# Forgetting attention with values stationary and heads on column halves; memory attention with three buffers, taken ahead of banks; a planner cost for accumulator reads

## The chip, the cores and the metric

One core of a Trainium2 chip runs the whole program in one launch. The metric is the device time of one execution in microseconds (us).

## The reference, cut to what matters

Three mixers, each followed by a gated feed-forward block, all in float32, on 256 tokens of width 1024 (one batch). Mixers 0 and 1 hold a main attention (retention, differential attention) beside a *memory attention*; mixer 2 holds a state-space part (SSD) beside the *forgetting attention* ("fox"). The two attentions that the change touches:

```python
def memory_attention(qc, mk, mv):            # 4 heads of 64, 256 memory rows; mixers 0 and 1
    sc = jnp.einsum('bshd,bmhd->bhsm', qc, mk) * (qc.shape[-1] ** -0.5)
    p = jax.nn.softmax(sc, axis=-1)
    return jnp.einsum('bhsm,bmhd->bshd', p, mv)

def fox_mixer(q, k, v, f_raw, ...):          # 16 heads of 64; mixer 2
    ...
    for start in range(0, s, Q_BLOCK):       # two query blocks of 128; keys 0:end
        logits = jnp.einsum('bhqd,bhkd->bhqk', qh[:, :, start:end], kh[:, :, :end]) * scale
        logits = logits + cum[:, :, start:end, None] - cum[:, :, None, :end]
        p = jax.nn.softmax(jnp.where(causal, logits, -jnp.inf), axis=-1)
        outs.append(jnp.einsum('bhqk,bhkd->bhqd', p, vh[:, :, :end]))

x = x + jnp.concatenate([o_main, o_mem], axis=-1) @ w_out[layer]     # mixers 0, 1
x = x + jnp.concatenate([y_ssd, y_fox], axis=-1) @ w_out_2           # mixer 2
```

## The kernel before, in words

**Work of TensorE.** Nearly all of it is products of activations with weights. Each is done as three matmuls of 512 columns in fp32r, on numbers that are split into a high and a low part: `wh` by `lth`, `wl` by `lth`, `wh` by `ltl`. A unit of weights is loaded into a stage `st` (4 buffers), cast on ScalarE (ACT) to `wh` (6 buffers), and subtracted on VectorE (DVE) to `wl`; the stage is free after that, and the next load into it is issued on SyncE. `lth` is a rounded copy of the activations made on ACT, `ltl` the rest made on DVE (`split`, L293). These matmuls, here called main matmuls, run back to back; the attentions' small matmuls (plain f32) are put between them. The stages are mixer 0, feed-forward 0, mixer 1, feed-forward 1, mixer 2, feed-forward 2; each mixer ends in an output projection (`w_out`, L958), which goes over pieces of 128 rows of the concatenated heads in the orders OUT0 = OUT1 = (4, 6, 0, 2) and OUT2 (L1304). A number in these lists is the first of two neighbouring pieces, so the memory heads (6, 7) come second of four in mixers 0 and 1.

**What sets the order.** A planner in Python (`Weave`, L102) writes one fixed sequence for each engine. Pieces of work are generators; the planner keeps a clock for each engine from the costs in `cost` (L116), and starts a generator's next step when its inputs are done on these clocks and its buffers (`yield ring, n`) are free. Casts of weights are put in as `fill` (L382). On the chip each engine runs its sequence strictly in order, and semaphores hold it where the inputs are late. So the costs decide the order alone, and a wait on the chip stops all that stands behind it on that engine. Every operation is recorded by one helper at L89, so the rows tell lines apart by names: `psm` (3 banks) and `psa` (5 banks) are PSUM.

**Memory attention** (`mem_attn`, L686). For each of two blocks of 128 queries: scores into two `psa` banks, two maxima on DVE, four exps on ACT with the row sums as `accum_out` into `mp` (ring of 2), four scalings on ACT by the reciprocal sums, eight transposes in two banks and two copies to `mpT` on ACT. Block 1 is started 2.5 us after block 0 by the planner's clock. After both, the values `mv` are the stationary operand and `mpT` streams 256 columns; the two heads of a pair write partitions 0 to 63 and 64 to 127 of one bank, that is, they take the two column halves of the array. The bank is split into `lth` and `ltl`, which the output projection reads as pieces 6 and 7.

**Forgetting attention** (`fox`, L1406, once for each half of the 16 heads). A `pair` of heads makes two `att`, one for each query block: scores, mask, maxima, exps with `accum_out` into `pr`, transposes (2 for the first block, 4 for the second), a copy to `pT`, then two or four matmuls with `pT` stationary and 64 columns of `vv` streaming, and a DVE multiply by the reciprocal sums into `fy`. When all four pairs are done, `fy` is transposed (4 for each token block), and split into `lth`/`ltl` in pieces of 512 columns.

Of the kernel before, what the change touches and what calls it, by code (L numbers as in the profile page):

```python
# [9 lines left out]
AF = mybir.ActivationFunctionType  # L10
ALU = mybir.AluOpType
# [3 lines left out]
P = 128  # L15
# [84 lines left out]
class Weave:  # L100
# [15 lines left out]
    def cost(self, key, op, args, kw, aps):  # L116
        n = max(a.size() // a.shape[0] if callable(a.size) else a.size // a.shape[0] for a in aps[:2])
        if key == "T":
            if op == "transpose":
                return 109  # L120
            return n / 2.4 + 3 if args[2].dtype == F32R else max(n / 0.6, 104) + 3
        if key == "V":
            return 65 + 1.05 * n + 60 * any(a.size() == a.shape[0] if callable(a.size) else a.size == a.shape[0] for a in aps[1:])
        if key == "S":
            c = 45 + 0.88 * n + 93 * sum(isinstance(kw.get(k), bass.AP) for k in ("bias", "scale", "accum_out"))
            func = args[2] if op == "activation" else None
            if func in (AF.Exp, AF.Silu) and func != self.table:
# [95 lines left out]
def _build(tc, a, out, stop):  # L223
# [462 lines left out]
    def mem_attn(l, mx, got, kvt, qc, oT, mpr):  # L686
# [14 lines left out]
        pT = mx.tile([P, 2, 4, 256], F32, tag="mpT", name=W.name("mpT"))  # L701

        def block(t):
            yield psa, 2
            sc = [psa.get(True), psa.get(True)]
            for p in range(2):
                for j in range(2):
                    T.matmul(sc[j][:, p * 256 : (p + 1) * 256], qT[64 * j : 64 * j + 64, p, t * P : (t + 1) * P],
                             kT[64 * j : 64 * j + 64, p, :], start=True, stop=True)
            prs = []  # L710
            yield
            for j in range(2):
                mxv = small([P, 2])
                V.tensor_reduce(mxv, sc[j][:].rearrange("p (j m) -> p j m", j=2), axis=AX.X, op=ALU.max)
                V.tensor_scalar(mxv, mxv, -0.125, None, op0=ALU.mult)
                yield mpr, 1
                pr = mpr.get(True)
                for p in range(2):
                    S.activation(pr[:, p * 256 : (p + 1) * 256], sc[j][:, p * 256 : (p + 1) * 256], AF.Exp,
                                 bias=mxv[:, p : p + 1], scale=0.125, accum_out=sums[:, t, 2 * p + j : 2 * p + j + 1])  # L720
                psa.close(sc[j])
                prs.append(pr)
            yield
            rs = small([P, 4])
            V.reciprocal(rs, sums[:, t, :])
            yield
            for j in range(2):
                for p in range(2):
                    cols = slice(p * 256, (p + 1) * 256)
                    S.activation(prs[j][:, cols], prs[j][:, cols], AF.Copy, scale=rs[:, 2 * p + j : 2 * p + j + 1])  # L730
            yield
            for j in range(2):
                yield psa, 1
                tp = psa.get(True)
# [273 lines left out]
    def mixer0(H, nxt, first):  # L1008
# [2 lines left out]
        w = a["w_in"][0]  # L1011
        u, E, oT = {}, {}, {}
        dtab = mx.tile([P, 6, 384], F32, name="dtab")
        sTr, hsq, onr, mpr = ring(mx, 384, "sT", 3), ring(mx, 512, "hsq", 1), ring(mx, 512, "on", 3), ring(mx, 512, "mp", 2)
        sqm[0] = ring(mx, 256, "sqm", 2)

        def chunk(c, ev, first=None):
# [112 lines left out]
    def mixer1(H, nxt, kv1):  # L1130
# [3 lines left out]
        oT, u, qkT, E = {}, {}, {}, {}  # L1134
        btab = mx.tile([P, 384], F32, name="btab")
        uqr, sqg, pdr, aTr = ring(mx, 512, "uq", 4), ring(mx, 512, "sqg", 1), ring(mx, 384, "pd", 6), ring(mx, 384, "aT", 5)
        hsq, onr, mpr = ring(mx, 512, "hsq", 1), ring(mx, 512, "on", 2), ring(mx, 512, "mp", 2)
        sqm[0] = ring(mx, 256, "sqm", 1)

        def chunk(c, serial=False):  # L1140
# [165 lines left out]
    def mixer2(H, nxt):  # L1306
# [11 lines left out]
        uxr = ring(mx, 1024, "ux", 2)  # L1318
        augr = {(i, t): ring(mx, (8, 66), f"aug{i}{t}", 1) for i in range(2) for t in range(2)}
        fTr = [Ring(W, mx, [66, 2, 256], F32, f"fT{i}", 2) for i in range(2)]  # L1320
        vvr, fyr, prr, pTr = ring(mx, 512, "vv", 2), ring(mx, 512, "fy", 2), ring(mx, 512, "pr", 3), ring(mx, 512, "pT", 2)
        tbr, dcr = ring(mx, 512, "tb", 1), ring(mx, 512, "dc", 4)
        aT = mx.tile([32, P], F32, name="aT")
        am = Ring(W, scr_pool, [32, P], F32, "am", 1).get(True)
# [80 lines left out]

        def fox(f, aug, deps, vv, got_v, pace):  # L1406
            sums = small([P, 2, 8], "f", 2)
            ys = [fyr.get(True) for _ in range(2)]

            def att(hp, ib, qT, kT):  # L1410
                nj = (ib + 1) * P
                yield psa, 1
                sc = psa.get(True)
# [13 lines left out]
                                 bias=mxv[:, j : j + 1], scale=0.125,  # L1427
                                 accum_out=sums[:, ib, 2 * hp + j : 2 * hp + j + 1])
                psa.close(sc)
                yield psa, 1  # L1430
                nb = 2 * (ib + 1)
                tp = psa.get(True)
                transposes(tp, blocks(pr, nb))
                prr.close(pr)
                yield pTr, 1
                pT = pTr.get(True)
                S.copy(pT[:, : nb * P], tp[:, : nb * P])
                psa.close(tp)
                yield psa, 1
                o = psa.get(True)  # L1440
                for j in range(2):
                    h = 2 * hp + j
                    for kb in range(ib + 1):
                        T.matmul(o[:, j * 64 : (j + 1) * 64], pT[:, (j * (ib + 1) + kb) * P : (j * (ib + 1) + kb + 1) * P],
                                 vv[kb][:, h * 64 : (h + 1) * 64], start=kb == 0, stop=kb == ib)
                pTr.close(pT)
                rs = small([P, 2])
                V.reciprocal(rs, sums[:, ib, 2 * hp : 2 * hp + 2])
                yield
                V.tensor_tensor(g64(ys[ib][:, 2 * hp * 64 : (2 * hp + 2) * 64]), g64(o[:, :P]), bcast(rs, 64), op=ALU.mult)  # L1450
                psa.close(o)
                yield

            def pair(hp):
# [15 lines left out]
                        for t in range(2):  # L1470
                            augr[which, t].close(aug[which][t])
                yield
                a0 = go(att(hp, 0, *qk))
                yield pace / 3
                a1 = go(att(hp, 1, *qk))
                yield [a0, a1]
                for which in range(2):
                    fTr[which].close(qk[which])

            yield deps + [got_v]  # L1480
            hs = []
# [2 lines left out]
                yield pace  # L1484
            yield hs
            vvr.close(*vv)
            lts = []
            for t in range(2):
                yield psa, 1
                ps = psa.get(True)  # L1490
                transposes(ps, blocks(ys[t]))
                fyr.close(ys[t])
                yield
                lt = yield from lt_tiles()
                yield from split(lt[0][:], lt[1][:], ps[:])
                psa.close(ps)
                lts.append(lt)
                for b in range(4):
                    oT[8 + 4 * f + b, t] = tuple(z[:, b * P : (b + 1) * P] for z in lt)
            yield  # L1500
            return lts


        def xbc_proj(i):
# [384 lines left out]
```

## Time and profile before

| | |
|---|---|
| median of 3 runs | 1014.52 us (1013.83 to 1016.05) |
| the profiled execution's own time | 1014.46 us |
| its span, first to last instruction | 1012.5 us |
| busy: PE, DVE, ACT, POOL | 99%, 67%, 61%, 7% of the span |

A row of the trace's timeline gives the start, the duration and the number of instructions of one kind in a run. Neighbouring matmuls overlap in their records, so the time that one takes from the engine is read as the distance from its start to the start of the next row, here called its step; the same holds for neighbouring rows of ACT. An f32 matmul is recorded as two passes.

### The profile page before, as it was taken

How to read it: one execution, taken by the hardware profiler on the slowest of the kernel's cores; microseconds unless marked ns; L12 is line 12 of the kernel's file. 1: busy time of each engine (PE TensorE's matmuls, PEld its weight loads, DVE VectorE, ACT ScalarE, POOL GpSimd, SP SyncE). 2: the span in 40 equal slices, each digit the busy share in tenths (PEclk: the TensorE clock that was granted, in tenths of full speed). 3: DMA queues.
4: the chain of work that ended last, by engine and by line, in shares of the span. 5: the costliest groups of instructions: out<-in, count | busy, mean ns of one | idle time of the engine just before them, and what ended most of it. 6: DMA issues, size and time to landing. Idle time of an engine off the chain costs nothing.

```text
span 1012.5 us, 13836 instructions
## 1 busy us (share of the span) xinstructions
PE 1002.2 (99%) x4994; PEld 832.4 (82%) x4994; DVE 678.1 (67%) x1026; ACT 622.5 (61%) x1001; POOL 69.8 (7%) x93
## 2 busy tenths in 40 slices
PE   8999999999999999999999999999999999999998
PEld 6887888888898777788888888888888888888887
DVE  5675666555556877756565477778767667878775
ACT  7558654443455887644445356688778557767853
POOL 1121000000001231100000001100400010000000
PEclk9999999999999999999999999999999999999999
DMA  7763566776564433677677457633632659877743
GB/s 250 261 222 105 183 208 212 252 229 193 179 227 155 146 104 107 208 247 233 203 229 239 137 152 220 215 104 104 210 125 84 208 164 289 262 232 240 247 156 116
DMA packets 121780, 193.79 MB, mean 191 GB/s; under 512 B 8400, under 2 KB 39920, under 8 KB 121584
## 3 DMA queue, kind: packets, MB, share of 16 engines
q1 hardware_dynamic: 121712, 192.92, 59.9%
q8 instruction: 39, 0.64, 0.3%
q14 instruction: 29, 0.24, 0.1%
HBM read 183.43 MB, written 9.45 MB: 191 GB/s over the span
## 4 chain that ended last, share of the span: by engine, by line
PE 91%; ACT 2%; DVE 2%; DMA 2%; POOL 2%; issue 1%; SPq 0%; ACTq 0%; DVEq 0%
PE psm L89 60%; PE psa L89 31%; POOL s8r L89 1%; DMA xt<-x 1%; ACT pd L89 1%; DMA dc<-am 1%; DMA st<-w_gate_up 1%; DVE wl L89 0%; DVE pd L89 0%; DVE s L89 0%; ACT wh L89 0%; POOL s4r L89 0%; POOL s16r L89 0%; SPq L259 0%; ACT qkT L89 0%
## 5 line engine op out<-in xcount | busy, mean ns | idle before, releaser
L89 DVE TENSOR_TENSOR wl<-st,wh 128x1024 fp32r<-128x1024 f32 (+2 forms) x339 | 388.4, 1166 | 195.4 <-ACT wh L89 194.5
L89 ACT CAST wh<-st 128x1024 fp32r<-128x1024 f32 (+2 forms) x339 | 334.5, 1007 | 223.9 <-PE psm L89 84.0
L89 PE MATMUL psm<-wh,lth 128*128 128x512 f32 (+2 forms) x1024 | 395.2, 386 | 1.1 <-ACT lth L89 1.1
L89 PE MATMUL psm<-wl,lth 128*128 128x512 f32 (+2 forms) x1024 | 385.6, 377 | 0.0
L89 PE MATMUL psm<-wh,ltl 128*128 128x512 f32 (+2 forms) x1024 | 381.0, 377 | 0.3 <-DVE ltl L89 0.2
L89 PEld LDWEIGHTS psm<-wh,ltl 128*128 128x128 f32 x1024 | 192.6, 188 | 36.8 <-DVE ltl L89 0.9
L89 PEld LDWEIGHTS psm<-wh,lth 128*128 128x128 f32 x1024 | 192.8, 188 | 35.8 <-issue 2.0
L89 PEld LDWEIGHTS psm<-wl,lth 128*128 128x128 f32 x1024 | 192.9, 188 | 32.6 <-DVE wl L89 0.7
L89 PE MATMUL psa<-wh,lth 128*128 128x512 f32 x328 | 130.7, 398 | 0.0
L89 PE MATMUL psa<-wl,lth 128*128 128x512 f32 x328 | 127.9, 390 | 0.0
L89 PE MATMUL psa<-wh,ltl 128*128 128x512 f32 x328 | 105.1, 390 | 0.0
L89 PEld LDWEIGHTS psa<-wh,ltl 128*128 128x128 f32 x328 | 61.6, 188 | 13.2
L89 PEld LDWEIGHTS psa<-wh,lth 128*128 128x128 f32 x328 | 61.6, 188 | 12.4 <-ACT lth L89 0.3
L89 PEld LDWEIGHTS psa<-wl,lth 128*128 128x128 f32 x328 | 61.7, 188 | 12.0 <-issue 0.2
L89 POOL TENSOR_SCALAR s1n<-s1n 128x1 f32<-128x1 f32 x14 | 5.6, 402 | 461.6 <-ACT sq L89 461.4
L89 DVE SCALAR_TENSOR_TENSOR cc<-na,ccol,cc 128x255 f32<-128x255 f32 (+1 forms) x64 | 27.4, 480 | 7.4 <-ACT cc L89 7.2
L89 ACT ACT_TABLE_LOAD x20 | 25.7, 1283 | 7.8 <-DMA dc<-am 2.8
L89 DVE SCALAR_TENSOR_TENSOR sg<-psm,s1n,sg 128x512 f32<-128x512 f32 (+1 forms) x24 | 16.9, 705 | 19.5 <-PE psm L89 19.3
L89 ACT ACTIVATE uu<-psm,s1n 128x512 f32<-128x512 f32 (+1 forms) x24 | 15.6, 652 | 18.3 <-PE psm L89 18.2
L89 ACT ACTIVATE sg<-psm,s1n 128x512 f32<-128x512 f32 (+1 forms) x24 | 15.7, 653 | 17.9 <-PE psm L89 17.7
L89 ACT ACTIVATE sq<-xt 128x512 f32<-128x512 f32 x24 | 15.2, 634 | 18.2 <-DVE xt L89 17.7
L89 POOL TENSOR_TENSOR s16r<-s16r,mhalf 128x16 f32<-128x16 f32 x7 | 22.2, 3166 | 0.6
(213 smaller groups left out, 829.3 us busy)
## 6 DMA issues: line engine op xcount, KB each, us to landing
st<-w_gate_up SPq DMA_DIRECT2D x80, 512.0 KB, 4.6
st<-w_in SPq DMA_DIRECT2D x67, 512.0 KB, 4.3
st<-w_down SPq DMA_DIRECT2D x66, 512.0 KB, 5.5
st<-w_up SPq DMA_DIRECT2D x40, 512.0 KB, 4.8
st<-w_out SPq DMA_DIRECT2D x32, 512.0 KB, 3.9
scr<-sq SPq DMA_DIRECT2D x64, 128.0 KB, 4.8
fl<-scr SPq DMA_DIRECT2D x16, 512.0 KB, 5.9
st<-w_in SPq DMA_DIRECT2D x30, 256.0 KB, 3.8
```

What stands on the lines that cost most here:

```text
L89: f(*args, **kw)
```

## The change

- In `cost`, an ACT operation with `accum_out` counts 110 ns more. It alters no instruction, only the planner's clock and so the order, in all stages.
- Memory attention: the `mp` ring has three buffers in place of two, and a block takes its two `mp` buffers first and its two score banks after that. Before, it took the banks first and each buffer after the maxima.
- Forgetting attention: the probabilities are scaled by the reciprocal sums on ACT (two instructions for each `att`) before they are transposed, `pT` holds both query blocks of a pair (768 columns, ring of three), and one set of matmuls for a pair has the values stationary and streams `pT`: 256 columns with the first 128 keys, 128 columns with the second, the two heads on the two column halves. Its result is the transposed one, so the `fy` multiplies on DVE and the 16 `fy` transposes are gone; it is split into `lth`/`ltl` in pieces of 256 columns.

```diff
@@ cost
             c = 45 + 0.88 * n + 93 * sum(isinstance(kw.get(k), bass.AP) for k in ("bias", "scale", "accum_out"))
+            c += 110 * ("accum_out" in kw)
@@ mem_attn, block(t)
+            yield mpr, 2
+            prs = [mpr.get(True), mpr.get(True)]
             yield psa, 2
             sc = [psa.get(True), psa.get(True)]
...
-                yield mpr, 1
-                pr = mpr.get(True)
+                pr = prs[j]
@@ mixer0, mixer1
-        hsq, onr, mpr = ring(mx, 512, "hsq", 1), ring(mx, 512, "on", 2), ring(mx, 512, "mp", 2)
+        hsq, onr, mpr = ring(mx, 512, "hsq", 1), ring(mx, 512, "on", 2), ring(mx, 512, "mp", 3)
@@ mixer2
-        vvr, fyr, prr, pTr = ring(mx, 512, "vv", 2), ring(mx, 512, "fy", 2), ring(mx, 512, "pr", 3), ring(mx, 512, "pT", 2)
+        vvr, prr, pTr = ring(mx, 512, "vv", 2), ring(mx, 512, "pr", 3), ring(mx, 768, "pT", 3)
@@ fox, att(hp, ib, qT, kT, pT)
+                rs = small([P, 2])
+                yield
+                V.reciprocal(rs, sums[:, ib, 2 * hp : 2 * hp + 2])
+                yield
+                for j in range(2):
+                    S.activation(pr[:, j * nj : (j + 1) * nj], pr[:, j * nj : (j + 1) * nj], AF.Copy, scale=rs[:, j : j + 1])
                 yield psa, 1
...
-                        T.matmul(o[:, j * 64 : (j + 1) * 64], pT[:, (j * (ib + 1) + kb) * P : (j * (ib + 1) + kb + 1) * P],
-                                 vv[kb][:, h * 64 : (h + 1) * 64], start=kb == 0, stop=kb == ib)
-                V.tensor_tensor(g64(ys[ib][:, 2 * hp * 64 : (2 * hp + 2) * 64]), g64(o[:, :P]), bcast(rs, 64), op=ALU.mult)
@@ fox, pair(hp)
+                        T.matmul(o[64 * j : 64 * j + 64, kb * P : 256], vv[kb][:, (2 * hp + j) * 64 : (2 * hp + j + 1) * 64],
+                                 pT[:, 384 * j + 256 * kb : 384 * j + 256 + 128 * kb], start=kb == 0, stop=kb == 1)
...
+                yield from split(lt[0][:, at : at + 256], lt[1][:, at : at + 256], o[:, :256])
@@ fox, end
-                transposes(ps, blocks(ys[t]))
-                yield from split(lt[0][:], lt[1][:], ps[:])
```

How the order moves is shown at three places, in rows as they stand in the fixed sequence of an engine; a name ends in a number that tells its buffers apart, `x2` means two like instructions.

The first is ACT in the output projection of mixer 0, from the last two copies of the transposed memory probabilities (`mpT`) on. Before (`lth_1152` is the memory heads' operand, `lth_1146` and `lth_1169` are the retention heads'):

```order
L89 COPY mpT_931<-psa_1107 128x4x128
L89 CAST wh_1117<-st_898 128x1024
L89 CAST wh_1119<-st_920 128x1024
L89 ACTIVATE lth_1146<-psa_1127,pcol 128x2x128 x2
L89 CAST lth_1152<-psa_1132 128x512
L89 ACTIVATE lth_1169<-psa_1141,pcol 128x2x128 x2
L89 CAST wh_1176<-st_947 128x1024
```

With the change (`lth_1198` is the memory heads' operand):

```order
L89 COPY mpT_931<-psa_1153 128x4x128
L89 CAST wh_1178<-st_949 128x1024
L89 CAST wh_1182<-st_1089 128x1024
L89 CAST wh_1188<-st_1137 128x1024
L89 CAST wh_1194<-st_1141 128x1024
L89 CAST lth_1198<-psa_1169 128x512
```

On PE at the same place the sequence now is:

```order
L89 MATMUL psa_1153<-pcol,mp_1022 128x128 x4
L89 MATMUL psa_1093<-wh_932,lth_874 128x512
L89 MATMUL psa_1169<-mpT_931,mv_577 64x256 x2
L89 MATMUL psa_1169<-mpT_931,mv_578 64x256 x2
L89 MATMUL psm_1091<-wh_1101,lth_1198 128x512
```

Six main matmuls with `wh_932` and `wh_1066` lie between the first and the third of these rows (one of them is shown). Before, twelve main matmuls and four transposes stood between the value matmuls and the first use of the memory heads' `lth`; now none stands there, and four weight casts stand ahead of `lth` on ACT.

The second is the same place of mixer 1, on ACT, with the change (`pd` is the differential attention's probabilities, `aT` their transposed difference; `lth_3769` is the memory heads' operand):

```order
L89 COPY mpT_3437<-psa_3690 128x4x128
L89 ACTIVATE pd_3681,s4s_3670<-pd_3681,s_830_3669 128x128
L89 ACTIVATE pd_3683,s4s_3670<-pd_3683,s_830_3669 128x256
L89 COPY mpT_3437<-psa_3714 128x4x128
L89 COPY aT_3729<-psa_3724 128x384
L89 CAST wh_3731<-st_3505 128x1024
L89 CAST wh_3733<-st_3532 128x1024
L89 CAST wh_3748<-st_3607 128x1024
L89 CAST wh_3754<-st_3702 128x1024
L89 ACTIVATE pd_3681<-pd_3681,s4s_3670 128x128
L89 ACTIVATE pd_3681<-pd_3681,s4s_3670 128x256
L89 CAST lth_3769<-psa_3737 128x512
```

Two more exps of `pd` lie between the two copies to `mpT`. Before, the copies were followed by 10 exps and scalings of `pd` and an evacuation of `u`, and `lth` came ahead of the next casts, with 24 main matmuls on PE between the value matmuls and its first use. On PE the value matmuls are now followed by seven transposes and then by the first main matmul that reads `lth_3769`.

The third is ACT in mixer 2's first half, with the change (`zs` are gates of the SSD part, `cv` its convolution, `pr` the forgetting attention's probabilities):

```order
L89 CAST wh_6355<-st_6138 128x1024
L89 ACTIVATE zs_6175<-psm_6177,s1n_5422 128x512
L89 ACTIVATE pr_6371,s16f_5996<-psa_6349,s_1407_6362 128x128 x2
L89 ACTIVATE zs_6176<-psm_6189,s1n_5531 128x512
L89 ACTIVATE pr_6402,s16f_5996<-psa_6368,s_1412_6381 128x256 x2
L89 CAST wh_6408<-st_6184 128x1024
L89 ACTIVATE pr_6443,s16f_5996<-psa_6399,s_1425_6416 128x128 x2
L89 CAST wh_6450<-st_6243 128x1024
L89 ACTIVATE pr_6371<-pr_6371,s_1410_6374 128x128 x2
L89 ACTIVATE pr_6402<-pr_6402,s_1421_6405 128x256 x2
```

A table load stands at each of the three switches between `zs` and `pr`. Before, the cast for the same unit of weights stood ahead of the convolution's activations and of both `zs`; now it stands behind them.

## Rows read from the trace of the kernel before

**Rows 1.** The page: busy time, the granted TensorE clock by slices of the span, and the chain that ended last.

```profile
PE 1002.2 (99%) x4994; PEld 832.4 (82%) x4994; DVE 678.1 (67%) x1026; ACT 622.5 (61%) x1001; POOL 69.8 (7%) x93
PEclk9999999999999999999999999999999999999999
PE 91%; ACT 2%; DVE 2%; DMA 2%; POOL 2%; issue 1%; SPq 0%; ACTq 0%; DVEq 0%
```

**Rows 2.** What PE waited for, in the whole span: us in total, times, longest.

```profile
PE psm L89 <- ACT lth L89: 1.1, 1, 1.1
PE psa L89 <- DVE u L89: 1.0, 1, 1.0
PE psa L89 <- DVE pd L89: 0.3, 1, 0.3
PE psa L89 <- DVE on L89: 0.2, 1, 0.2
```

**Rows 3.** Timeline of PE in mixer 2: start, duration, operation, count.

```profile
668.25 0.55 PE L89 MATMUL psa<-vv,pT 128*128 128x64 f32 x4
668.61 0.48 PE L89 MATMUL psm<-wh,lth 128*128 128x512 f32 x1
669.83 1.00 PE L89 MATMUL psa<-vv,pT 128*128 128x64 f32 x8
670.66 0.61 PE L89 MATMUL psa<-pcol,ux 128*128 128x128 f32 x4
...
698.14 1.02 PE L89 MATMUL psa<-tb,bct 128*128 128x512 f32 x2
699.00 0.60 PE L89 MATMUL psa<-pcol,fy 128*128 128x128 f32 x4
699.36 0.47 PE L89 MATMUL psm<-wh,lth 128*128 128x512 f32 x1
```

**Rows 4.** Timeline of PE in the output projection of mixer 0, around the memory attention's value matmuls.

```profile
106.18 0.60 PE L89 MATMUL psa<-pcol,on 128*128 128x128 f32 x4
106.71 1.95 PE L89 MATMUL psa<-mpT,mv 128*64 128x256 f32 x16
108.59 0.66 PE L89 MATMUL psa<-pcol,on 128*128 128x128 f32 x4
109.00 0.47 PE L89 MATMUL psa<-wh,lth 128*128 128x512 f32 x1
...
111.85 0.39 PE L89 MATMUL psm<-wh,lth 128*128 128x512 f32 x1
```

**Rows 5.** Timeline of ACT there; in brackets the idle time ahead and what ended it.

```profile
104.99 0.59 ACT L89 COPY mpT<-psa 128x512 f32<-128x512 f32 x1 [0.65 <-PE psa L89]
105.47 1.99 ACT L89 CAST wh<-st 128x1024 fp32r<-128x1024 f32 x2
107.37 0.84 ACT L89 ACTIVATE lth<-psa,pcol 128x256 fp32r<-128x256 f32 x2
108.71 0.59 ACT L89 CAST lth<-psa 128x512 fp32r<-128x512 f32 x1 [0.50 <-PE psa L89]
109.28 0.84 ACT L89 ACTIVATE lth<-psa,pcol 128x256 fp32r<-128x256 f32 x2
110.01 2.00 ACT L89 CAST wh<-st 128x1024 fp32r<-128x1024 f32 x2
113.76 1.05 ACT L89 CAST wh<-st 128x1024 fp32r<-128x1024 f32 x1 [1.75 <-DMA st<-w_out]
```

**Rows 6.** Timeline of ACT in the output projection of mixer 1.

```profile
386.03 0.42 ACT L89 ACTIVATE pd<-pd,s 128x128 f32<-128x128 f32 x1
...
387.80 0.68 ACT L89 ACTIVATE u<-psm,s1n 128x512 f32<-128x512 f32 x1
...
391.00 0.78 ACT L89 ACTIVATE pd<-pd,s4s 128x128 f32<-128x128 f32 x2
391.69 0.56 ACT L89 CAST lth<-psa 128x512 fp32r<-128x512 f32 x1
...
395.22 0.85 ACT L89 COPY aT<-psa 128x384 f32<-128x384 f32 x2
```

**Rows 7.** Busy time by windows of mixer 2's attention stage (us; windows with their length, then PE, PEld, DVE, ACT, POOL, granted clock, DMA share, GB/s).

```profile
650.00:675.00 25.00, 25.00 (x155) 21.45 (x154) 16.42 (x44) 22.24 (x48) 0.00 (x0) 1.00 0.23 68
675.00:700.00 25.00, 25.00 (x144) 21.02 (x144) 20.95 (x46) 22.67 (x44) 0.00 (x0) 1.00 0.36 104
700.00:725.00 25.00, 24.91 (x133) 20.98 (x132) 20.71 (x33) 17.89 (x32) 5.90 (x6) 1.00 0.53 158
725.00:750.00 25.00, 24.87 (x135) 20.50 (x134) 16.16 (x42) 16.66 (x34) 5.25 (x4) 1.00 0.64 202
750.00:775.00 25.00, 25.00 (x148) 21.36 (x148) 20.19 (x47) 23.63 (x48) 0.00 (x0) 1.00 0.28 97
775.00:800.00 25.00, 25.00 (x137) 20.94 (x136) 19.21 (x31) 15.10 (x27) 0.98 (x2) 1.00 0.42 140
```

**Rows 8.** Timeline of ACT in mixer 0 (the scalings of the memory attention) and in mixer 2 (the cast of a unit of weights), and of PE at that unit's first use.

```profile
99.56 1.71 ACT L89 ACTIVATE mp<-mp,s 128x256 f32<-128x256 f32 x4
101.29 1.28 ACT L89 ACT_TABLE_LOAD   x1
...
680.32 1.04 ACT L89 CAST wh<-st 128x1024 fp32r<-128x1024 f32 x1
...
697.36 0.48 PE L89 MATMUL psm<-wh,lth 128*128 128x512 f32 x1
```

More of the change, by code (lines that the diff above doesn't have):

```diff
@@ L709, in block @@
                              kT[64 * j : 64 * j + 64, p, :], start=True, stop=True)
-            prs = []
             yield
@@ L721, in block @@
                 psa.close(sc[j])
-                prs.append(pr)
             yield
@@ L1013, in mixer0 @@
         dtab = mx.tile([P, 6, 384], F32, name="dtab")
-        sTr, hsq, onr, mpr = ring(mx, 384, "sT", 3), ring(mx, 512, "hsq", 1), ring(mx, 512, "on", 3), ring(mx, 512, "mp", 2)
+        sTr, hsq, onr, mpr = ring(mx, 384, "sT", 3), ring(mx, 512, "hsq", 1), ring(mx, 512, "on", 3), ring(mx, 512, "mp", 3)
         sqm[0] = ring(mx, 256, "sqm", 2)
@@ L1407, in fox, with att @@
             sums = small([P, 2, 8], "f", 2)
-            ys = [fyr.get(True) for _ in range(2)]
-            def att(hp, ib, qT, kT):
+            lts = {}
+            def att(hp, ib, qT, kT, pT):
                 nj = (ib + 1) * P
@@ L1429, in att @@
                 psa.close(sc)
[L1430 to L1443, printed above, removed]
-                        T.matmul(o[:, j * 64 : (j + 1) * 64], pT[:, (j * (ib + 1) + kb) * P : (j * (ib + 1) + kb + 1) * P],
-                                 vv[kb][:, h * 64 : (h + 1) * 64], start=kb == 0, stop=kb == ib)
-                pTr.close(pT)
                 rs = small([P, 2])
+                yield
                 V.reciprocal(rs, sums[:, ib, 2 * hp : 2 * hp + 2])
                 yield
-                V.tensor_tensor(g64(ys[ib][:, 2 * hp * 64 : (2 * hp + 2) * 64]), g64(o[:, :P]), bcast(rs, 64), op=ALU.mult)
-                psa.close(o)
+                for j in range(2):
+                    S.activation(pr[:, j * nj : (j + 1) * nj], pr[:, j * nj : (j + 1) * nj], AF.Copy, scale=rs[:, j : j + 1])
+                yield psa, 1
+                tp = psa.get(True)
+                transposes(tp, blocks(pr, 2 * (ib + 1)))
+                prr.close(pr)
+                S.copy(pT[:].rearrange("p (j n) -> p j n", j=2)[:, :, ib * P : ib * P + nj],
+                       tp[:, : 2 * nj].rearrange("p (j n) -> p j n", j=2))
+                psa.close(tp)
                 yield
@@ L1472, in pair @@
                 yield
-                a0 = go(att(hp, 0, *qk))
+                yield pTr, 1
+                pT = pTr.get(True)
+                a0 = go(att(hp, 0, *qk, pT))
                 yield pace / 3
-                a1 = go(att(hp, 1, *qk))
+                a1 = go(att(hp, 1, *qk, pT))
                 yield [a0, a1]
@@ L1478, in pair @@
                     fTr[which].close(qk[which])
+                yield psa, 1
+                o = psa.get(True)
+                for kb in range(2):
+                    for j in range(2):
+                        T.matmul(o[64 * j : 64 * j + 64, kb * P : 256], vv[kb][:, (2 * hp + j) * 64 : (2 * hp + j + 1) * 64],
+                                 pT[:, 384 * j + 256 * kb : 384 * j + 256 + 128 * kb], start=kb == 0, stop=kb == 1)
+                pTr.close(pT)
+                if hp // 2 not in lts:
+                    lts[hp // 2] = yield from lt_tiles()
+                lt, at = lts[hp // 2], hp % 2 * 256
+                yield from split(lt[0][:, at : at + 256], lt[1][:, at : at + 256], o[:, :256])
+                psa.close(o)
+                for t in range(2):
+                    oT[8 + 4 * f + hp, t] = tuple(z[:, at + t * P : at + (t + 1) * P] for z in lt)
+                yield
             yield deps + [got_v]
@@ L1486, in fox @@
             vvr.close(*vv)
[L1487 to L1490, printed above, removed]
-                transposes(ps, blocks(ys[t]))
-                fyr.close(ys[t])
-                yield
-                lt = yield from lt_tiles()
-                yield from split(lt[0][:], lt[1][:], ps[:])
[L1496 to L1501, printed above, removed]
+            return [lts[0], lts[1]]
         def xbc_proj(i):
```

## The prediction

> **What bounds the kernel now.** [...] Then PE's waits: the longest that other engines cause in the middle of the program are 1.1, 1.0, 0.3 and 0.2 us [rows 2]; the order of before leaves almost nothing to win there, and a new order can only put waits in. Third, the timelines at the places that the change touches, for the price of a step of work on PE and ACT [rows 3 to 6], and fourth the busy time by windows in mixer 2, to see whether ACT has room for the scalings that it is given [rows 7]. The sum is made against the profiled execution, 1014.46 us, which is 0.06 us under the median of the runs. I call a difference under 0.2%, 2.0 us, no change, for the runs of before spread over 2.2 us.
>
> **Forgetting attention on PE: less work.** Before, a pair of heads takes four passes of 64 columns for its first query block and eight for its second. From the start of each burst to the start of the next row these are 0.36 us (668.25 to 668.61) and 0.83 us (669.83 to 670.66) [rows 3], so 1.19 us a pair and 9.5 us for eight pairs. The new form is not in mixer 2, but it is in mixers 0 and 1: values stationary, 256 columns streamed, two heads on the two column halves. There 16 passes take 1.88 us (106.71 to 108.59) [rows 4]. One f32 pass of 512 columns takes 0.43 us alone (two from 698.14 to 699.00) [rows 3], so 256 columns take 0.215 us, and 16 in a row would be 3.44 us. That they take 1.88 us shows that the halves run two at a time: 8 x 0.215 = 1.72 us, and 0.16 us over. The four transposes ahead of them start at 106.18 and take about 0.43 us where nothing follows them at once (0.36 us from 699.00 to 699.36 in mixer 2 [rows 3]), which leaves some 0.1 us ahead as well [rows 4]; I put 0.24 us for entering and leaving the form. A pair is now two double passes of 256 columns and two of 128: 2 x 0.215 + 2 x 0.108 + 0.24 = 0.89 us, 7.1 us for eight pairs. That is **-2.4 us**. If the halves ran one after the other here, a pair would be 4 x 0.215 + 4 x 0.108 + 0.24 = 1.53 us, 12.3 us in all, 2.8 us more than before; nothing in the edit differs from the form that runs two at a time, so I take the first, and keep the other as an end.
>
> [...]
>
> The 16 transposes of fy go: 0.36 us for four [rows 3], **-1.4 us**. The number of transposes of pr is the same. The DVE multiplies into fy go as well; DVE was not what PE waited for in this stage, so they are counted at nothing. The split of the result is done in eight pieces of 256 columns in place of four of 512, on ACT and DVE, behind the last pair; it is off PE.
>
> **Memory attention and the account: a new order.** No instruction of PE goes or comes in mixers 0 and 1. What changes is when block 1 starts: it takes both of its buffers first, with three in the ring it has to wait for one that block 0 gives back at its first transposes, and it runs later. The order shows what this does. In mixer 0 the value matmuls now stand directly ahead of the main matmul that reads their result, and on ACT four casts of weights stand between the last copy to mpT and lth. The value matmuls start when that copy is done. From there ACT takes four casts and the split: two casts take 1.90 us (105.47 to 107.37), so 0.95 us each, and the lth cast 0.57 us (108.71 to 109.28) [rows 5]: 4 x 0.95 + 0.57 = 4.37 us. PE has 1.88 us of its own work in that time [rows 4]. It stands for 4.37 - 1.88, with 0.1 us of hand-over about **2.4 us** if the copy is the last to arrive, and 1.8 us if the copy was done while PE was still on the six main matmuls ahead (the copy is then hidden, and ACT is 0.7 us earlier). If no cast lay between, it would still stand for the split, some 0.7 us. If the third or fourth cast waits for its weights, as one did here for 1.75 us [rows 5], it is more: up to 4 us. Just ahead of this the transposes of the retention heads and of mp follow the last projection at once, where before they had main matmuls between: I put 0.6 us for these, so **+3.0 us** in mixer 0 (1.9 to 4.6).
>
> In mixer 1 it is the same, with more on ACT: after the copy come aT, at 0.43 us (two from 395.22, 0.85 us), four casts, two scalings of pd, at 0.69 us (391.00 to 391.69), and lth at 0.56 us [rows 6]: 0.43 + 3.8 + 0.69 + 0.56 = 5.5 us. PE has the value matmuls, 1.88 us [rows 4], and seven transposes, some 0.8 us, so it stands 2.8 us. The last copy itself stands behind four exps of pd with their reads, which took 1.77 us before (386.03 to 387.80) [rows 6]; the value matmuls wait for that copy, and I take 1.0 us of it as not covered. Another transposed head is late once, 0.4 us. Against that go the waits of before at these places, for u, pd and on, 1.5 us [rows 2]. **+2.7 us** (1.9 to 4.5). The feed-forward blocks keep their order, and I count nothing there.
>
> **Forgetting attention on ACT: more work.** The change adds 16 scalings of 128 columns and 16 of 256. Four of 256 columns take 1.73 us (99.56 to 101.29) [rows 8], 0.43 us each; two of 128 take 0.69 us [rows 6], 0.35 us each. That is 12.5 us, 6.2 us in each half. From 650 to 700 us ACT is busy 44.9 of 50 us [rows 7], and all exps of the first half lie there: 51.1 us of work in 50. From 750 to 775 it is busy 23.6 of 25 us [rows 7], and ten of the second half's sixteen exps lie there: 3.9 more, 27.5 us of work in 25. What covered this is the lead of the weight casts: the unit cast at 680.32 is used at 697.36, 16 us after the cast's end [rows 8]. In the new order that cast stands behind both zs, the convolution's activations and three table loads at 1.28 us each [rows 8], so the lead is spent. PE then meets late casts or a late evacuation: 51.1 - 50 = 1.1 us and, of the 2.5 us of the second half, 1.5 us, since ACT had idle time just ahead of it. **+2.6 us** (0, where the lead lasts, to 6.0, where only the room that the windows of 650 to 700 and 750 to 775 us show, 5.1 + 1.4 us, covers the 12.5).
>
> [...]
>
> **Sum.** -2.4 - 1.4 + 3.0 + 2.7 + 2.6 = +4.5 us: 1014.46 + 4.5 = **1019.0 us**.
>
> **The rivals.**
> - *Both stages better than I read them* (no change). The lead of the casts lasts through mixer 2, and the two joins are at their low ends: -3.8 + 1.9 + 1.9 + 0.5 = +0.5, 1015.0 us (1012.7 to 1016.5). For it: the casts had 16 us of lead. Against: both windows overflow.
> - *The joins are covered, and the change is faster.* This is one mechanism: PE reaches the value matmuls of both mixers so late, for some other wait or since ACT runs ahead, that the four casts are done. It decides from the point at which ACT is over 4 us ahead of PE at the last mpT copy. Then only the split stands, 0.7 us each, the waits of before in mixer 1, 1.5 us, are gone, and the fox stage keeps its 3.8 us less 0.5: 1014.46 - 3.8 + 1.4 - 1.5 + 0.5 = 1011.1 us (1010.0 to 1012.4). Against: the last transposes for that copy are only six main matmuls ahead on PE, and the buffers of two of the casts are freed by these same matmuls.
> - *ACT or the column halves decide mixer 2* (slower by more). The weights are late by the scalings less the room that covers them, 6.0 us in place of 2.6: 1022.4 us; or the halves run one after the other, 12.3 - 7.1 = 5.2 us more than in my sum: 1024.2 us (1022 to 1027 for the case). For it: 51.1 and 27.5 us in windows of 50 and 25. Against: the halves that run two at a time in [rows 4].
> - That the edit does not do what it says in PE's work is the end with halves in turn, above. For a clock that falls in a wait of 3 us no row speaks: the longest wait shown in the middle is 1.1 us, with the clock in its top tenth [rows 1, 2].
>
> **How the numbers follow.** My forecast has 0.59, with a range of its own of 1016.5 to 1022.0 us; no change 0.20; covered joins 0.12; the worse mixer 2 0.09. The range from 1012.7 to 1022.5 leaves out most of the last two, 0.19. Faster by over 0.2% is the third case, 0.12; within 0.2% are the second and the low edge of the forecast's own case, 0.22; slower is the rest, 0.66.
>
> **What the profile after would show.** Right: PE idle for 2 us or more ahead of a main matmul, put down to ACT lth, near 113 us and again near 390 us; the vv matmuls as bursts of eight passes of a little under 0.9 us, with no fy rows; ACT over 95% busy in 680 to 700 and 750 to 775 us, and PE idle there by ACT wh, DVE wl, or a bank that ACT evacuates. Wrong: no wait for lth at the two joins (then the casts were early); bursts of over 1.4 us (then the halves run in turn); PE at 25.00 of 25 us through mixer 2 (then the lead lasted), or waits in the feed-forward blocks, for which I have no term.

## The result and the profile after

The changed kernel takes 1025.62 us (median of 4 runs, 1022.88 to 1027.97) where the kernel before takes 1015.09 (median of 4): ratio 1.0104, 95% interval 1.0079 to 1.0129. It is slower, as forecast, but by 10.5 us where 4.5 were forecast, and outside the range. The profiled execution took 1027.97 us, with a span of 1026.0 us and a mean clock of 0.994; it is the slowest of the four, 2.4 us over the median. Against the span of before it is 13.5 us longer. Medians leave out the executions in a slower state, of which run 5 has one (1433.63 us) and the kernel before two. A *stand* is a time in which PE stands still; a *join* is the place at which an output projection first reads the memory heads' `lth`.

The page of the changed kernel, busy times and the chain that ended last; they answer to [rows 1]:

```profile
PE 1004.3 (98%) x4946; PEld 827.9 (81%) x4946; DVE 675.0 (66%) x1014; ACT 633.5 (62%) x1037; POOL 68.0 (7%) x93
PE 89%; ACT 4%; DVE 2%; DMA 2%; issue 1%; POOL 1%; SPq 0%; ACTq 0%; DVEq 0%
```

PE has 48 instructions fewer and is busy 2.1 us longer all the same: an instruction counts as busy longer where the clock is low (behind the first stand below, at a granted clock of 0.50, a main matmul's record is 0.63 us, and at 1.00 it is 0.39). What PE waited for (us in total, times, longest), where before had nothing over 1.0 us in the middle (the 1.1 us of [rows 2] stands at 6.6 us, at the start, and those rows leave out 0.9 us for `xt` at 412.7 us):

```profile
PE psm L89 <- ACT lth L89: 3.0, 1, 3.0
PE psm L89 <- ACT zs L89: 3.0, 1, 3.0
PE psa L89 <- DVE pd L89: 2.9, 1, 2.9
...
PE psa L89 <- ACT lth L89: 1.3, 1, 1.3
PE psm L89 <- ACT wh L89: 1.0, 1, 1.0
PE psa L89 <- ACT xd L89: 1.0, 1, 1.0
...
PE psm L89 <- DVE wl L89: 0.8, 1, 0.8
```

The places one by one. In the output projection of mixer 0 (timelines of PE and of ACT; the last number in brackets is idle time and what ended it), which answers to [rows 4, 5]:

```profile
111.46 1.95 PE L89 MATMUL psa<-mpT,mv 128*64 128x256 f32 x16
116.42 0.79 PE L89 MATMUL psm<-wh,lth 128*128 128x512 f32 x1 [3.01 <-ACT lth L89]
117.01 0.63 PE L89 MATMUL psm<-wl,lth 128*128 128x512 f32 x1
117.44 0.63 PE L89 MATMUL psm<-wh,lth 128*128 128x512 f32 x1
...
120.80 0.40 PE L89 MATMUL psa<-wh,lth 128*128 128x512 f32 x1
121.04 0.39 PE L89 MATMUL psa<-wl,lth 128*128 128x512 f32 x1
```

```profile
110.38 0.62 ACT L89 COPY mpT<-psa 128x512 f32<-128x512 f32 x1
110.84 2.99 ACT L89 CAST wh<-st 128x1024 fp32r<-128x1024 f32 x3
114.83 1.04 ACT L89 CAST wh<-st 128x1024 fp32r<-128x1024 f32 x1 [1.00 <-DMA st<-w_out]
115.78 0.58 ACT L89 CAST lth<-psa 128x512 fp32r<-128x512 f32 x1
```

The copy, four casts and the split stand in a row as the order said, and the fourth cast waits 1.00 us for its weights, with the split behind it, which starts at 115.78 us. Behind the stand, main matmuls start 0.43 us apart (117.01 to 117.44), and a little later 0.24 us apart (120.80 to 121.04): the granted clock was 0.50 from 116.5 to 119.5 us, and 1.00 from 120 to 122 us. At the join of mixer 1, PE waits for the last copy to `mpT`, and then for `pd`, whose scalings stand behind four casts on ACT (two rows of PE, two of ACT):

```profile
399.62 1.95 PE L89 MATMUL psa<-mpT,mv 128*64 128x256 f32 x16 [0.76 <-ACT mpT L89]
405.02 0.83 PE L89 MATMUL psa<-pcol,pd 128*128 128x128 f32 x3 [2.86 <-DVE pd L89]
...
399.84 4.06 ACT L89 CAST wh<-st 128x1024 fp32r<-128x1024 f32 x4
403.81 0.80 ACT L89 ACTIVATE pd<-pd,s4s 128x128 f32<-128x128 f32 x2
```

The windows around the two joins and in mixer 2 (length, then PE, PEld, DVE, ACT, POOL, granted clock, DMA share, GB/s) show where else it is low:

```profile
116.00:118.00 2.00, 1.58 (x4) 1.30 (x5) 1.60 (x2) 0.36 (x1) 0.00 (x0) 0.58 1.01 351
118.00:120.00 2.00, 2.00 (x7) 1.57 (x6) 0.22 (x1) 0.00 (x0) 0.00 (x0) 0.57 0.82 275
405.00:408.00 3.00, 2.91 (x11) 2.31 (x12) 2.76 (x4) 1.15 (x3) 0.00 (x0) 0.74 1.04 384
408.00:411.00 3.00, 3.00 (x17) 2.81 (x16) 0.14 (x1) 0.60 (x1) 0.00 (x0) 0.69 0.70 209
702.00:705.00 3.00, 2.26 (x5) 1.03 (x6) 3.00 (x6) 3.00 (x9) 0.00 (x0) 0.73 0.35 81
705.00:708.00 3.00, 3.00 (x15) 2.52 (x14) 1.93 (x4) 2.46 (x7) 0.00 (x0) 0.70 0.84 263
780.00:784.00 4.00, 4.00 (x23) 3.44 (x23) 1.94 (x5) 3.96 (x7) 0.00 (x0) 1.00 0.40 133
```

In each of the first three places the lost share of the clock, times the window, is 1.7 us: 2 x (0.42 + 0.43), 3 x (0.26 + 0.31), 3 x (0.27 + 0.30). The fourth stand, 3.0 us near 779 us for zs, is not followed by a low clock here.

By stage, from the time at which the residual is added at the end of each mixer and block, the profiled execution is later than that of before by 0.55 us at the start, and by 5.5 in mixer 0, 0.2 in feed-forward 0, 1.9 in mixer 1, 0.4 in feed-forward 1, 3.1 in mixer 2 and 1.9 in feed-forward 2. (A stage ends in four such additions, and this is read at the first. Read at the last, feed-forward 0 and 1 differ by 0.0 us: their 0.2 and 0.4 us belong to the ends of mixers 0 and 1.)

The new form on PE, in the second half of mixer 2; it answers to the vv rows of [rows 3]:

```profile
795.66 0.87 PE L89 MATMUL psa<-pT,vv 128*64 128x256 f32 x8
796.46 0.66 PE L89 MATMUL psa<-pcol,pr 128*128 128x128 f32 x4
```

A pair takes 0.80 us, where 1.19 stood before. The wait near 701 us, from the timeline of ACT: a cast stands behind two table loads, and PE waits 0.96 us for it and 0.76 us for its wl.

```profile
696.18 1.28 ACT L89 ACT_TABLE_LOAD   x1
697.48 0.69 ACT L89 ACTIVATE zs<-psm,s1n 128x512 f32<-128x512 f32 x1
698.18 1.28 ACT L89 ACT_TABLE_LOAD   x1
...
700.40 1.04 ACT L89 CAST wh<-st 128x1024 fp32r<-128x1024 f32 x1
```

The longest wait of mixer 2 is for `zs`, also behind a table load (ACT, then PE):

```profile
777.84 1.28 ACT L89 ACT_TABLE_LOAD   x1
779.14 0.69 ACT L89 ACTIVATE zs<-psm,s1n 128x512 f32<-128x512 f32 x1
...
779.88 0.50 PE L89 MATMUL psm<-wh,lth 128*128 128x512 f32 x1 [2.96 <-ACT zs L89]
```

### The profile page after: what moved, and what is told of

It reads as the page before. It is cut to its first block, busy times and chain, and to the rows that moved or that the text cites. A ratio compares the mean times of both kernels' runs of the same rounds, so it can differ in the third digit from the quotient of the medians.

```text
span 1026.0 us, 13746 instructions
## 1 busy us (share of the span) xinstructions
PE 1004.3 (98%) x4946; PEld 827.9 (81%) x4946; DVE 675.0 (66%) x1014; ACT 633.5 (62%) x1037; POOL 68.0 (7%) x93
## 4 chain that ended last, share of the span: by engine, by line
PE 89%; ACT 4%; DVE 2%; DMA 2%; issue 1%; POOL 1%; SPq 0%; ACTq 0%; DVEq 0%
PE psm L89 60%; PE psa L89 28%; DVE wl L89 1%; ACT L89 1%; ACT wh L89 1%; DMA fl<-scr 1%; DMA xt<-x 1%; DMA st<-w_out 0%; POOL s8r L89 0%; ACT cc L89 0%; ACT mp L89 0%; SPq L260 0%; DVE cc L89 0%; ACT cv L89 0%; POOL s2r L89 0%
```

## The experiments

Times are medians, ratios are to runs of the kernel before on the same chip; stages are read from the profiled executions.

**1 to 4: which part.** The change has three parts: the account, the memory attention's edit, the forgetting attention's form. The account was not run alone.

Against the changed kernel, run 3 takes the account out, run 4 the form; run 1 takes out the account and the memory edit, run 2 the account and the form:

```diff
@@ cost (out in runs 1, 2, 3)
-            c += 110 * ("accum_out" in kw)
@@ mem_attn, block(t) (out in run 1, with the third mp buffer)
-            yield mpr, 2
-            prs = [mpr.get(True), mpr.get(True)]
@@ fox (out in runs 2, 4: all hunks of mixer 2)
-                    S.activation(pr[:, j * nj : (j + 1) * nj], pr[:, j * nj : (j + 1) * nj], AF.Copy, scale=rs[:, j : j + 1])
...
```

> The kernel before with the forgetting attention's new form alone: no account of accumulator reads, memory attention as before, so the sequences of mixers 0 and 1 are those of before word for word. Theory A (the account's order puts waits into the joins of the output projections, and the clock falls behind the longest): no difference up to the end of feed-forward 1; in mixer 2 the form saves about 4 us of PE and meets waits of 1 to 5 us on ACT; 1012 to 1016 us. Theory B (the new form's load on ACT is what costs): mixer 2 is 3 us or more longer than before, 1017.5 us or more.

> The kernel before with the memory attention's edit alone (three buffers, taken ahead of the banks). In its order twelve main matmuls stay between the value matmuls and the first use of their operand in mixer 0, and more in mixer 1. Theory A: the buffers by themselves are harmless, 1013.5 to 1016.5 us, no wait of PE for ACT lth over 1.5 us. Theory B says the same. A third theory, C (taking the buffers first holds block 1 back and is what makes the join late): a wait of 2 to 3 us for lth in mixers 0 and 1, 1020 us or more.

> The changed kernel without the account: memory attention's edit and the new form of the forgetting attention. Theory A: the join waits of 3.0 and 2.9 us and the two clock falls behind them are gone, about 8 us less than the changed kernel up to feed-forward 1; mixer 2 as in the run of the form alone; 1012 to 1017 us. Theory B: 1017.5 us or more, all of it in mixer 2. Theory C: as slow in mixers 0 and 1 as the changed kernel, 1022 us or more.

> The account and the memory attention's edit, with the forgetting attention as before. Its sequences in mixers 0 and 1 are those of the changed kernel. Theory A: 8 us slower than before at the start of mixer 2 (6 where the clock does not fall), with the waits for lth and pd of about 3 us; mixer 2 at -1 to +4 us; 1020 to 1027 us. Theory B: no more than 4 us slower than before at the end.

| | us | ratio (95%) | mixer 0 | mixer 1 | mixer 2 | feed-forward 2 |
|---|---|---|---|---|---|---|
| e1 form | 1016.63 | 1.0016 (1.0006 to 1.0025) | +1.0 | -0.3 | +1.3 | +2.4 |
| e2 memory | 1026.93 | 1.0124 (1.0109 to 1.0139) | +2.0 | +10.8 | -0.8 | 0.0 |
| e3 both | 1030.87 | 1.0162 (1.0147 to 1.0177) | +1.4 | +10.7 | +1.1 | +1.4 |
| e4 account, memory | 1022.98 | 1.0083 (1.0062 to 1.0104) | +5.5 | +0.1 | +0.3 | +1.4 |
| all | 1025.62 | 1.0104 (1.0079 to 1.0129) | +6.0 | +1.9 | +3.1 | +1.9 |

(Mixer 0 holds the start's jitter, up to 1 us.) Theory A fell by runs 2 and 3, though run 4 came out in its range: beside the memory edit the account is not what hurts. Without it the memory edit costs 12 us, almost all in mixer 1 (3.4 us of that is two stretches at the lower clock), and the account takes 4 to 5 us of that back, by moving the harm to the join of mixer 0. What the account does alone is not shown. Theory C holds in its place as to the edit that costs; its price in mixer 0 and the wait that it named, for lth, were wrong. PE's waits with the memory edit alone:

```profile
PE psa L89 <- DVE on L89: 5.1, 2, 3.5
PE psm L89 <- ACT u L89: 3.0, 2, 1.7
PE psa L89 <- DVE pd L89: 1.7, 1, 1.7
```

In its order on ACT, the exps of pd for the last two heads stand behind the memory heads' lth and four casts; before, they stood ahead of both. ACT also waits 1.9 us there for their maxima from DVE, so the casts are not the whole of it; the rest of the chain was not followed. Theory B is half right: the form alone is no gain but a small loss, 1.3 us in mixer 2 (1.7 us of low clock included) and 2.4 us in a block that the form doesn't touch. Run 4, without the form, loses 1.4 us in that block too, and run 2, with neither the form nor the account, nothing: the form is enough for this loss, and so is the account beside the memory edit.

**5: is it the third buffer, or the order of taking?**

```diff
-        ..., ring(mx, 512, "mp", 2)
+        ..., ring(mx, 512, "mp", 3)
```

> The kernel before with three mp buffers in place of two and nothing else: a block still takes its banks first and each buffer after its maxima. Theory C (it is the order of taking, buffers first, that holds block 1 back): no harm, 1013.5 to 1016.5 us, block 1's scores where they were, no wait for lth, on or pd over 1.5 us. Rival D (the third buffer itself moves the order for the worse): 1020 us or more, as in the run of the edit alone (1026.9).

1015.24 us, ratio 1.0006 (0.9996 to 1.0016): no difference. So it is `yield mpr, 2` ahead of the banks that costs: with three buffers, of which each block takes two at once, block 1 waits for what block 0 gives back. The first exp of block 1 in mixer 0 starts at 95.3 us before, at 92.0 us in this run, and at 98.2 us in run 2, behind both copies of block 0 to mpT. A ring of four, from which both blocks could take two, was not run.

**6: the price of the clock.** The values' eight matmuls are issued once more, outside the planner's account.

```diff
                     T.matmul(ps[...], v[mb][...], pT[:, j, 2 * p + mb, :], start=mb == 0, stop=mb == 1)
+        for p in range(2):
+            for mb in range(2):
+                for j in range(2):
+                    T.eng.matmul(ps[...], v[mb][...], pT[:, j, 2 * p + mb, :], start=mb == 0, stop=mb == 1)
```

> The changed kernel with the memory attention's value matmuls issued twice into the same bank, in mixers 0 and 1, outside the planner's account, so that no sequence changes but for these. PE gets 1.9 us more work in each mixer, in a time in which it stood still for 3.0 and 2.9 us. Theory F (a stand of that length is followed by the lower clock, and costs that again): no row with a clock under 1.0 behind these two places, mean clock up by 0.002 to 0.004, and 2 to 4 us less than the changed kernel, 1021.5 to 1024 us. Rival G (the fall of the clock has nothing to do with the stand, or the work is added to the path): the clock falls as before, and the time is 1025.6 us or up to 3.8 us more.

The timeline of PE at the two joins:

```profile
112.43 1.90 PE L757 MATMUL psa<-mpT,mv 128*64 128x256 f32 x16
115.57 0.50 PE L89 MATMUL psm<-wh,lth 128*128 128x512 f32 x1 [1.24 <-ACT lth L89]
...
399.04 1.90 PE L757 MATMUL psa<-mpT,mv 128*64 128x256 f32 x16
402.38 0.83 PE L89 MATMUL psa<-pcol,pd 128*128 128x128 f32 x3 [0.86 <-DVE pd L89]
```

3.6 us more work on PE, stands of 1.24 and 0.86 us in place of 3.01 and 2.86, the clock at 1.00 behind both, and mixers 0 and 1 shorter than in the changed kernel by 1.6 us (2.4 with the start's jitter) and 1.9 us. The whole is 1024.25 us, ratio 1.0097 (1.0081 to 1.0113), which can't be told from the changed kernel's: in this profile the clock falls instead behind the stand for zs, to 0.50 from 774 to 776 us. So the total does not decide, and the price of a fall is shown rather than its cause: PE has as much more work as the stands are shorter, so the 1.6 and 1.9 us are the clock's. That the shorter stands kept the clock up is not shown, for run 7 has stands of 2.60, 2.58 and 2.95 us at the same places in its profile and no fall behind any. Its mixers 0, 1 and 2 are 2.1, 1.8 and 1.6 us shorter than the changed kernel's (of the first two, 0.4 and 0.3 us are shorter stands, and 0.2 us of the first is the start's jitter). The price in the whole time is seen between executions of one program: the four of run 7 have mean clocks of 1.000, 1.000, 0.995 and 0.993, and take 1020.70, 1020.79, 1025.83 and 1026.04 us; the one with the profile is the first. What decides whether a fall follows a stand stays open.

**7: feed-forward 2.**

```diff
             used(k0)
+            if w is a["w_out_2"] and k0 == 14:
+                S.activation(small([P, 1], "pre", 1), pc(C_FQ), AF.Silu)
```

> The changed kernel with one more ACT instruction: a Silu of one column in the output projection of mixer 2, behind its fifth pair of pieces, so that the table for the last feed-forward block's Silu is loaded there. Theory H (the 1.9 us that feed-forward 2 lost come from a table load of 1.28 us that now stands in its first gate, since mixer 2 now ends with an Exp and not a Silu): no table load in feed-forward 2, no wait of 1.3 us of PE for lth there, 1.3 to 1.9 us less than the changed kernel, 1023.5 to 1024.5 us. Rival: the wait stays, for the casts of weights stand ahead of lth.

Feed-forward 2 now takes 0.1 us more than before in place of 1.9, and its wait for lth is gone. The table load moved from 869.19 us in the changed kernel (first row) to the output projection (second row):

```profile
869.19 1.28 ACT L89 ACT_TABLE_LOAD   x1
```

```profile
819.91 1.28 ACT L89 ACT_TABLE_LOAD   x1
```

Theory H holds by the stage. The whole, 1023.31 us, ratio 1.0083 (1.0062 to 1.0104), can't decide it, since the four executions lie 5 us apart.

**8: scalings on DVE** (with the form alone and the table early).

```diff
-                    S.activation(pr[...], pr[...], AF.Copy, scale=rs[:, j : j + 1])
+                    V.tensor_scalar(pr[...], pr[...], rs[:, j : j + 1], None, op0=ALU.mult)
```

> The kernel before with the forgetting attention's new form alone, but with the 32 scalings by the reciprocal sums on DVE in place of ACT, and the table load of the last feed-forward block early. Theory I (in mixer 2 the new form saves its 3.8 us of PE and loses it to the ACT queue): ACT gets 12.5 us back, the wait for pr of 2.4 us and the clock fall behind it are gone, 2 to 5 us less than with the scalings on ACT: 1010.5 to 1013.5 us. Rival J (the loss is one of order, whichever engine scales): 1014.5 to 1017 us, with a wait of PE for another step of the same chain.

1017.66 us, ratio 1.0031 (1.0019 to 1.0043). Theory I fell: with ACT freed of all scalings PE stands 2.4 us for zs at 691 us where the form alone stood 2.4 us for pr at 696, and mixer 2 is 3.3 us longer than before (two stretches at the lower clock, 3.4 us, included). That the wait moved to another step is what rival J said, but the time is above its range too. Ahead of both waits ACT's timeline shows switches between Silu and Exp: six loads of 1.28 us in 14 us with the form alone, three in 8 us here. The last rows ahead of the wait of run 1 (ACT, then PE), and the wait of run 8:

```profile
692.70 1.28 ACT L89 ACT_TABLE_LOAD   x1
695.63 0.70 ACT L89 ACTIVATE pr<-pr,s 128x128 f32<-128x128 f32 x2
...
696.09 0.62 PE L89 MATMUL psa<-pcol,pr 128*128 128x128 f32 x2 [2.43 <-ACT pr L89]
```

```profile
691.49 0.50 PE L89 MATMUL psm<-wh,lth 128*128 128x512 f32 x1 [2.44 <-ACT zs L89]
```

Moving the scalings also moved the order, so this is no test of their load alone.

**9 to 12: the table switches.** In run 9 the gates' Silu is left out and only a scaled copy is done, issued past the planner, which still counts a Silu, so that the order is unchanged. In runs 10 to 12 it is done later, on both gates together:

```diff
-            return zs, proj(w, H, g * 512, 512, lambda t, ps, r: S.activation(zs[t][:], ps[:], AF.Silu, scale=r))
+            return zs, proj(w, H, g * 512, 512, lambda t, ps, r: S.activation(zs[t][:], ps[:], AF.Copy, scale=r))
@@ ssd
             yield [got_z]
+            for c in range(2):
+                S.activation(zs[c][:], zs[c][:], AF.Silu)
+            yield
```

> The forgetting attention's new form alone, with the SSD part's gates zs taken out of PSUM by a plain scaled copy where a Silu stood (the Silu of these gates is left out). The planner counts them as before, so every sequence is that of the form alone; but six of the 20 table loads of ACT fall away. Theory K (what eats the new form's saving in mixer 2 is the switching of ACT's table between Silu and Exp, 1.28 us each, which stands ahead of pr, casts and evacuations in turn): the wait of 2.4 us for pr and the clock fall behind it are gone, mixer 2 is 3 to 4 us shorter than before; the load in feed-forward 2 stays, with its 1.3 us wait: 1011.5 to 1013.5 us. Rival (the 32 scalings by themselves overfill ACT): 1015 us or more.

> The forgetting attention's new form alone, with zs taken out of PSUM by a scaled copy and its Silu done on both zs together ahead of their use: four more ACT instructions, four table loads fewer, and mixer 2 ends with a Silu, so that no load stands in feed-forward 2. Theory K: no wait of PE over 1.5 us in mixer 2 and feed-forward 2, mixer 2 3 to 4 us shorter than before, 1010.5 to 1012.5 us. Rival: a later step of the SSD part is late in its turn, 1014 us or more.

> The kernel before with the gates' Silu done late in the same way, and nothing of the change. PE had hardly a wait in this stage, so theory K says no difference, 1013.5 to 1016 us: the table switching costs only where ACT's cover is used up. Rival: it is faster by itself, and the run with the new form owes its gain to this: 1012 us or less.

> The whole change with the gates' Silu done late in the same way. Theory K: mixer 2 and feed-forward 2 give back what they cost (3.1 + 1.9 us) and the saving of the new form shows, about 3.5 us; the two joins in mixers 0 and 1 stay, with 3.0 and 2.9 us and the clock falls that come behind them: 1017 to 1020 us. Rival: 1022 us or more.

| | us | ratio (95%) | mixer 2 | feed-forward 2 |
|---|---|---|---|---|
| e9 form, gates without Silu | 1011.85 | 0.9971 (0.9961 to 0.9981) | -4.2 | +2.2 |
| e10 form, gates late | 1009.58 | 0.9947 (0.9934 to 0.9959) | -5.0 | 0.0 |
| e11 before, gates late | 1013.83 | 0.9994 (0.9985 to 1.0003) | -0.9 | 0.0 |
| e12 whole change, gates late | 1017.66 | 1.0028 (1.0017 to 1.0038) | -2.5 | 0.0 |

Three lie in the ranges of theory K, and run 10 is 0.9 us below its range. In run 9 the sequences, the scalings and ACT's other work are those of run 1, and four table loads of 18 are gone (not six of 20), all of them between 686 and 693 us: the wait of 2.4 us and the fall behind it go with them, and mixer 2 is 5.5 us shorter than in run 1. Run 11 shows that the late gates alone are worth nothing that can be measured. Nor are the loads a cost in themselves: the kernel before has five of them between 681 and 694 us, and PE has no wait there. So they cost only together with what the new form puts on the way to PE. And ACT's sum does not set the loss: run 10 has two loads fewer than run 1 and four more Silus, its ACT is as busy (run 1, then run 10), and PE has no such wait:

```profile
PE 1001.8 (99%) x4946; PEld 824.8 (81%) x4946; DVE 676.2 (67%) x1014; ACT 629.7 (62%) x1035; POOL 69.6 (7%) x93
PE 998.1 (99%) x4946; PEld 824.5 (82%) x4946; DVE 675.5 (67%) x1014; ACT 629.5 (62%) x1037; POOL 69.9 (7%) x93
```

Run 10 beats both kernels; PE's longest waits in it are at the start and those of before:

```profile
PE psa L89 <- DVE ones L89: 1.3, 1, 1.3
PE psa L89 <- DMA xt<-x: 1.2, 1, 1.2
PE psa L89 <- DVE u L89: 1.0, 1, 1.0
```

Run 12 keeps the two joins: stands of 3.1 and 2.6 us, and 6.4 us more than before at the start of mixer 2.

## Why the prediction was wrong in size

Three steps failed: the low clock behind a stand, which the sum put at nothing (5.1 us in the profiled execution); ACT in mixer 2, put down to the load of the scalings (waits of 5.6 us where 2.6 were put down); and feed-forward 2, put at nothing (1.9 us). Term by term:

- **The new form's matmuls** (-2.4): right. 0.80 us a pair against 0.89 put down; the two column halves run together. With the fy transposes the saving was put at 3.8 us; mixer 2 without the table switches is 4.2 us shorter, and by runs 10 and 11 the form is worth 5.0 - 0.9 = 4.1 us. From 1.19 to 0.80 us is a factor of 1.5.
- **The join of mixer 0** (+3.0): the mechanism was right, and the stand was 3.01 us with 0.41 us of another wait ahead of it. That the sum came out so near is partly luck: 1.00 us of the stand is the fourth cast's wait for its weights, which the prediction named but did not put in its sum, and the four casts and the split alone are worth 2.0 us. The 0.1 us of hand-over is the prediction's own estimate; here it is 0.06 us, from the end of `lth` at 116.36 us to the matmul at 116.42. What is missing is the 1.7 us of low clock behind it.
- **The join of mixer 1** (+2.7): stands of 0.76 us for mpT and 2.86 us for pd, with the four casts ahead of the scaling of pd, as worked out, though the wait stands one step earlier, at the transposes of pd and not at lth. Without the 1.7 us of the clock the stage is only 0.2 us longer than before (0.6 us by the last addition); waits of before that went account for some 2.3 us (u 0.97, pd, on, and 0.88 for xt behind the first addition, which the prediction didn't count), the rest isn't assigned to rows.
- **ACT in mixer 2** (+2.6): the place was right, the reason and the size were not. The waits sum to 0.96 + 0.76 + 0.96 + 2.96 = 5.6 us, and 1.7 us of clock come on top. The prediction laid it to the 12.5 us of scalings in full windows; taking all scalings off ACT (run 8) did not help, taking four table loads off it (run 9) did, and run 10 has no such wait with as much work on ACT as run 1. So, for the form alone, a row of loads of 1.28 us at the point where PE next needs that queue decides, and not the queue's sum, which is all that windows show. It does so in the new form only, since before had such rows without a wait; which of the new form's steps uses up the cover was not shown. In the change itself, run 12 takes mixer 2 from +3.1 to -2.5 us, and the waits of 2.96 us for zs and 0.96 us for wh are gone.
- **The feed-forward blocks** (0): right for 0 and 1, failed for 2. The order was taken to be unchanged; in fact mixer 2 now ends with an Exp and the next Silu's table load falls into feed-forward 2's first gate, 1.8 us (run 7).
- **The clock**: failed; it was named without a price, since no row of before showed a long wait. It was worth 3 x 1.7 = 5.1 us in the profiled execution, and about 5.2 us between executions of run 7's program. The four executions of the changed kernel have mean clocks of 0.994, 0.994, 0.998 and 0.996, so in its median it is less than in the profiled one.

So of the 9.0 us between the forecast's 4.5 and the profiled 13.5, 5.1 are the clock, 2.6 mixer 2 (more waits, less a somewhat larger saving), 1.9 feed-forward 2, 0.8 mixer 0, 0.6 the ends of mixers 0 and 1 behind their first addition, and 0.5 the start's jitter; mixer 1 was 2.5 us cheaper than its term.

## What to carry over

A fixed order that is nearly without waits is itself the asset: an edit should be priced by what it does to the sequences at the places where one stage's result is first read, and by the table that ACT holds at a stage's end (here a load of 1.28 us in the next stage, and 1.8 us of feed-forward 2), before its instructions are counted. A saving on the bounding engine can be lost to a lump in the queue that feeds it, as the new form's 4.1 us were in run 1; run 9 found the lump by taking it away in an unchanged order, where run 8, which took away load and changed the order, did not. A resource that is taken early holds whoever comes second, and here one more of it didn't help, since each user took two.

## What was not expected of the hardware

In these runs a stand of TensorE of 2.4 to 3.0 us was in some places followed by about 3 us at half the clock, which cost 1.7 us again: behind the stand of 3.01 us in the changed kernel the granted clock was 0.50 from 116.5 to 119.5 us, and behind that of 2.43 us in run 1 it was 0.61 and 0.54 in the two windows of 2 us from 698 to 702 us. The length of the stand alone did not decide it. At the join of mixer 0 stands of 3.0 us were followed by a fall in run 4 (0.50 from 118 to 120 us) and in the changed kernel, and one of 2.60 us in run 7 was not (1.00 from 116 to 130 us); at the join of mixer 1 the stand of 2.86 us in the changed kernel was (0.50 from 406.6 to 409.5 us), and those of 2.6 us in runs 4 and 7 were not (1.00 from 404 to 412 us in both); the stand of 2.96 us for zs in the changed kernel was not (1.00 from 780 to 784 us), and the like one in run 6 was (0.50 from 774 to 776 us). In the change's profile two stands of 0.96 and 0.76 us, with one matmul between them, were also followed by a fall (0.50 from 703.6 to 706.5 us), and in run 6 single stands of 1.24 and 0.86 us were not (1.00 from 116 to 120 and from 402 to 408 us). Why like stands at the same places pass without a fall in other runs no run here shows.
